# Second layer's MLP: six pairs ahead in shared PSUM banks, low parts behind the next sum, and the second product's weight sums one per step

## The chip, the cores and the metric

The kernel runs on one core of one Trainium2 chip. The metric is the time of one execution in microseconds of device time. The core has a matrix engine (TensorE, PE in the rows; its weight loads are PEld), a vector engine (VectorE, DVE), an activation engine (ScalarE, ACT), a general engine (GpSimd, POOL) and a queue of DMA issues (SyncE, SP). Each engine works through its own instructions in order.

## The reference

A backbone of two layers over 1024 latent tokens of width 1024. Layer 0 mixes tokens by attention, layer 1 by a gated linear attention; each layer ends with a modulated norm and an MLP of width 4096 with squared ReLU. The change touches the MLP of layer 1 alone:

```
h = modulate(rmsnorm(x, g), shift, scale)       # 1024 x 1024
x = x + gate * (relu(h @ w1) ** 2 @ w2)         # w1 1024 x 4096, w2 4096 x 1024
```

All is float32.

## The kernel before

**Numbers in two parts.** For a matmul each f32 operand is split into a rounded high part (`rounded`, a cast on ACT, L164) and a low part, operand minus high part (a subtraction on VectorE, L170). `mm3` (L203 to L205) multiplies high by high, high by low and low by high into one PSUM bank. So a product of 128 outputs over four blocks of 128 is 12 matmuls, 128x512 each.

**Seven products for eight.** `FastMlp` computes both products of the MLP by the Strassen-Winograd scheme: each matrix is cut in 2x2, and from sums of the quarters seven products (steps A11, A12, S1, S2, S3, S4, A22; `STEPS`, L60) are enough. The right-hand operands of the first product are the combinations "11", "21", "22", T1 to T4 of the quarters of the normed input. `combine` (L1216) makes T1 to T4 on VectorE, `shifted` (L1198) makes the others; each is then split. The weight sums S1 = A21 + A22, S2 = S1 − A11, S3 = A11 − A21, S4 = A12 − S2 are made in `add_up` (L1339) on VectorE and split in `prepare` (L1352). Steps A11 and A12, S1 and S2, and so on share sums: `took` (L1291) takes each result out of PSUM, adds what belongs together (`square`, L1274, adds and squares with ReLU on VectorE), subtracts hidden quarters for the second product (`sub`, L1286) and stores them (`store`, L1289) to a buffer `hsp` in DRAM.

**Order.** All engines of this part run in written order (`run`, L1509). There are 16 pairs of 128 hidden columns each.

- `beside` (L1236) makes "11" and "21" for the first half of the norm during the projection before.
- `begin` (L1361): with LEAD = 4 (L70), pairs 0 to 3 run A11 and A12 while the second half of the norm comes in (`norm.begin`, `norm.end`), then S1 and S2 as T1 and T2 become ready. Each product has a PSUM bank of its own; A11's result is copied by ACT (L1299), and VectorE adds it to A12's.
- `first` (L1431): the led pairs' S3, S4, A22, then all seven steps of each pair from 4 on. At fixed distances from the end (`nearly`) it begins to load hidden quarters (`fetch`, L1490) and w2 (`load_rows`, L1467), and to split them.
- `all` (L1516): the second product, four chunks of four pairs by seven steps (`STEPS2`), each step four groups g of 12 matmuls. Behind each group stand, on VectorE, the group before's addition into x (`add`, an STT, L1547) and one piece of the next step's operands (`made`, L1501: `weight`, L1476, then splits W and B). In the S2 step `weight` makes all four sums of a pair (L1481 to L1484).

Of the kernel before, what the change touches and what calls it, by code (L numbers as in the profile page):

```python
# [15 lines left out]
P = 128  # L16
# [45 lines left out]
STEPS2 = STEPS[:5] + (STEPS[6], STEPS[5])  # L62
# [7 lines left out]
LEAD = 4  # L70
# [25 lines left out]
def kernel(  # L96
# [1075 lines left out]
    class FastMlp:  # L1172
# [5 lines left out]
        def __init__(self, l, lead):  # L1178
            self.l, self.lead = l, lead
            self.B = {c: [None] * 4 for c in COMBOS}  # L1180
            self.ts, self.hids = {}, {}
            self.raw, self.sums, self.ops = {}, {}, {}

# [32 lines left out]
        def combine(self, c, j):  # L1216
            b2 = self.norm.ab[0][1][:, j + 4:j + 5]
            (t11, t21), (t12, t22) = [[self.ts[i, j][:, e] for e in range(2)] for i in range(2)]
            v = nc.vector

            if c == "T1":
                self.T[j] = tmp([512], n="T")
                v.tensor_sub(self.T[j], t12, t11)
                split(self.operand(c, j), self.T[j])
            elif c == "T2":
                v.scalar_tensor_tensor(t11, t22, b2, self.T.pop(j), op0=ALU.add, op1=ALU.subtract)
                split(self.operand(c, j), t11)
            elif c == "T3":
                v.scalar_tensor_tensor(t12, t22, self.db[:, j:j + 1], t12, op0=ALU.add, op1=ALU.subtract)
                split(self.operand(c, j), t12)  # L1230
            else:
                v.scalar_tensor_tensor(t21, t21, b2, t11, op0=ALU.add, op1=ALU.subtract)
                split(self.operand(c, j), t21)
                del self.ts[0, j], self.ts[1, j]

        def beside(self, norm, d):  # L1236
# [14 lines left out]
            if d >= 6:  # L1251
                for p in range(self.lead // 2 * (d - 6), self.lead // 2 * (d - 5)):
# [6 lines left out]
        def product(self, ps, w, c, start):  # L1259
            for j in range(4):  # L1260
# [30 lines left out]
        def took(self, p, c, ps):  # L1291

            led = p < self.lead
# [3 lines left out]
            if c == "A11":  # L1297
                h.s1 = h.at("T4") if led else tmp([512], n="s1")
                nc.scalar.copy(h.s1, ps)  # L1299
            elif c == "A12":  # L1300
                h.square("11", ps, h.s1)
            elif c == "S1":
                h.u4 = h.at("T2") if led else tmp([512], n="p5")
                nc.scalar.copy(h.u4, ps)
            elif c == "S2":
# [4 lines left out]
                else:  # L1310
                    h.u2 = tmp([512], n="u2")
                    nc.scalar.copy(h.u2, ps)
# [9 lines left out]
            else:  # L1322
                h.square("21", ps, h.u2 if led else None)
# [28 lines left out]
        def prepare(self, p, c):  # L1352
            t = slot([2, 512], F32R, n="W")
            self.ops[p, c] = (t[:, 0], t[:, 1])
            split(self.ops[p, c], self.sums[p, c] if c[0] == "S" else self.quarter(p, c))
# [5 lines left out]
        def begin(self):  # L1361

            norm, lead = self.norm, self.lead
            self.T = {}

            def early(p):
                w = W.take(min(lead - 1 - p, 1))
                for e, c in ((0, "A11"), (1, "A12")):
                    ps = bank([512])
                    self.product(ps, (w[0][:, e * 512:e * 512 + 512], w[1][:, e * 512:e * 512 + 512]),  # L1370
                                 ("11", "21")[e], True)
                    yield lambda p=p, c=c, ps=ps: self.took(p, c, ps)
# [6 lines left out]
            a0, a1 = early(0)  # L1379
            norm.begin(1)  # L1380
            a0()
            b0, = [next(e1 := early(1))]
            norm.end(1)
            a1()
            b1 = next(e1)
            for j in range(4):
                self.scaled(1, j)
            b0()
            for j in (0, 1):
                self.combine("T1", j)  # L1390
            b1()
            for j in (2, 3):
                self.combine("T1", j)
            for p in range(2, lead):
                late = list(early(p))
                for j in ((4, 5), (6, 7))[p - 2]:
                    self.scaled(1, j)
                for t in late:
                    t()
            self.spill(1)  # L1400
            for p in range(lead):
                self.raw[p, 0] = raws.tile([P, 1024], F32, name=nm("raw"), tag="raw")
                nc.sync.dma_start(self.raw[p, 0][:, :512], w1[self.l, 2 * p][:, :512])

            for p in range(lead):
                t = middle("S1", "T1", p)
                self.combine("T2", p)
# [678 lines left out]
```

## Time and profile before

| | us |
|---|---|
| median of 3 runs | 2946.93 (2946.42 to 2947.62) |
| the profiled execution | 2947.68 |
| its span | 2946.0 |
| first product of this MLP, TensorE | about 2222 to 2576 |
| second product, TensorE | about 2576 to 2928 |

The span is the time from the first to the last instruction that the profile shows; 1.7 us of the execution lie around it. In the rows further down, "busy" counts work, "x" instructions, and the bracket at the end of a row tells how long the engine stood idle before it and which instruction released it. Lines are those of the kernel before.

### The profile page before, as it was taken

The numbers are of one execution on the slowest core, as the hardware profiler recorded it, in microseconds if no ns is written. First come the engines' busy times: TensorE is split into PE (matmuls) and PEld (weight loads), VectorE is DVE, ScalarE is ACT, GpSimd is POOL, SyncE is SP. The second block draws the span as 40 slices with busy tenths as digits, with TensorE's granted clock in tenths as the row PEclk, the third lists the DMA queues.
The fourth block names the chain that finished last, engine by engine and source line by source line (L and its number), as shares of the span: only waits on it lengthen the run. The fifth ranks groups of instructions, "written<-read, shape, count | busy, mean of one in ns | idle before, by whom it ended". The sixth has DMA issues, their size and how long they took to land.

```text
span 2946.0 us, 38543 instructions
## 1 busy us (share of the span) xinstructions
PE 2771.4 (94%) x14728; PEld 2370.0 (80%) x14728; DVE 1985.7 (67%) x3321; ACT 1205.3 (41%) x2353; POOL 661.6 (22%) x600
## 2 busy tenths in 40 slices
PE   5998999999799999999999999999998699999987
PEld 3987899978688888888888889987786588877776
DVE  7858788887877655555455633546766877777776
ACT  4534677773432322321221425875532233333332
POOL 4236455533322422300000100135400111100000
PEclk9999999999899999999999999999999899999998
DMA  6231000044222323311111212334342544553422
GB/s 236 84 103 62 14 15 14 15 140 175 72 79 91 110 86 100 100 51 36 36 43 37 79 55 78 119 139 147 126 164 72 185 150 148 211 217 139 146 83 72
DMA packets 109049, 296.89 MB, mean 101 GB/s; under 512 B 10721, under 2 KB 24161, under 8 KB 108865
## 3 DMA queue, kind: packets, MB, share of 16 engines
q1 hardware_dynamic: 93520, 242.00, 24.3%
q0 software_dynamic: 15344, 52.44, 5.0%
q8 instruction: 115, 1.88, 0.3%
q14 instruction: 70, 0.57, 0.1%
HBM read 229.39 MB, written 65.01 MB: 100 GB/s over the span
## 4 chain that ended last, share of the span: by engine, by line
PE 66%; issue 12%; DVE 12%; ACT 4%; POOL 3%; DMA 2%; SPq 0%; POOLq 0%; DVEq 0%; ACTq 0%
PE b L203 19%; PE b L204 19%; PE b L205 19%; PE b L882 2%; PE b L867 2%; DVE adaj L331 1%; PE b L457 1%; POOL hsp L1289 1%; POOL adaj L317 1%; DMA ada<-in_adaT 1%; DVE wlo L170 1%; DVE B L170 1%; DMA hr<-hsp 1%; DVE h L279 1%; PE b L1749 1%
## 5 line engine op out<-in xcount | busy, mean ns | idle before, releaser
L203 PE MATMUL b<-h,whi 128*128 128x512 f32 (+1 forms) x1544 | 562.8, 366 | 4.3 <-ACT h L164 2.5
L204 PE MATMUL b<-h,whi 128*128 128x512 f32 (+1 forms) x1544 | 560.9, 364 | 3.7 <-DVE h L279 2.2
L205 PE MATMUL b<-h,wlo 128*128 128x512 f32 (+1 forms) x1544 | 560.4, 363 | 4.1 <-DVE wlo L170 4.1
L203 PE MATMUL b<-B,W 128*128 128x512 f32 (+1 forms) x880 | 348.7, 396 | 49.7 <-ACT B L164 25.9
L204 PE MATMUL b<-B,W 128*128 128x512 f32 (+1 forms) x880 | 347.2, 395 | 2.3 <-DVE B L170 2.3
L205 PE MATMUL b<-B,W 128*128 128x512 f32 (+1 forms) x880 | 345.8, 393 | 0.9 <-DVE W L170 0.9
L204 PEld LDWEIGHTS b<-h,whi 128*128 128x128 f32 x1544 | 293.5, 190 | 52.0 <-DVE h L170 3.4
L203 PEld LDWEIGHTS b<-h,whi 128*128 128x128 f32 x1544 | 293.0, 190 | 52.1 <-ACT h L164 4.4
L205 PEld LDWEIGHTS b<-h,wlo 128*128 128x128 f32 x1544 | 293.1, 190 | 51.1 <-DVE wlo L170 6.0
L1153 DVE SCALAR_TENSOR_TENSOR x<-b,mod,x 128x512 f32<-128x512 f32 (+1 forms) x384 | 248.6, 659 | 116.7 <-PE b L205 114.4
L317 POOL TENSOR_TENSOR adaj<-ada,sc 128x1024 f32<-128x1024 f32 x80 | 218.4, 2746 | 383.5 <-PE b L205 186.2
L203 PE MATMUL b<-hid,whi 128*128 128x512 f32 (+1 forms) x768 | 272.9, 355 | 0.0
L204 PE MATMUL b<-hid,whi 128*128 128x512 f32 (+1 forms) x768 | 272.1, 354 | 0.0
L205 PE MATMUL b<-hid,wlo 128*128 128x512 f32 (+1 forms) x768 | 271.9, 354 | 0.0
L203 PEld LDWEIGHTS b<-B,W 128*128 128x128 f32 x880 | 169.9, 193 | 91.1 <-ACT B L164 31.0
L1122 DVE TENSOR_TENSOR relu<-relu 128x512 f32<-128x512 f32 (+1 forms) x96 | 79.6, 835 | 195.3 <-ACT relu L1115 195.3
L204 PEld LDWEIGHTS b<-B,W 128*128 128x128 f32 x880 | 170.0, 193 | 40.7 <-DVE B L170 6.6
L318 ACT ACTIVATE adaj<-adaj 128x1024 f32<-128x1024 f32 x80 | 84.8, 1060 | 288.2 <-POOL adaj L317 288.1
L205 PEld LDWEIGHTS b<-B,W 128*128 128x128 f32 x880 | 169.6, 193 | 35.3 <-DVE W L170 1.6
L170 DVE TENSOR_TENSOR wlo<-raw,whi 128x1024 fp32r<-128x1024 f32 x118 | 150.6, 1283 | 45.4 <-ACT whi L164 43.9
L203 PEld LDWEIGHTS b<-hid,whi 128*128 128x128 f32 x768 | 145.5, 190 | 20.5 <-issue 0.2
L204 PEld LDWEIGHTS b<-hid,whi 128*128 128x128 f32 x768 | 145.4, 189 | 20.3 <-issue 0.2
(284 smaller groups left out, 5632.6 us busy)
## 6 DMA issues: line engine op xcount, KB each, us to landing
raw<-in_w SPq DMA_DIRECT2D x136, 512.0 KB, 3.9
ada<-in_adaT SPq DMA_DIRECT2D x96, 512.0 KB, 4.1
hr<-hsp SPq DMA_DIRECT2D x56, 512.0 KB, 4.5
hsp<-hid POOLq DMA_DIRECT2D x48, 512.0 KB, 4.0
raw<-in_od_win SPq DMA_DIRECT2D x25, 512.0 KB, 3.6
x<-in_xT SPq DMA_DIRECT2D x20, 512.0 KB, 8.2
xsp<-x SPq DMA_DIRECT2D x16, 512.0 KB, 3.3
x<-xsp SPq DMA_DIRECT2D x16, 512.0 KB, 9.1
```

The costliest lines, as they stand in the source:

```text
L170: (lo or nc.vector).tensor_sub(dst[1], src, f(dst[0]))
L203: nc.tensor.matmul(ps, lhsT=ah, rhs=bh, start=start, stop=False, skip_group_check=more)
L204: nc.tensor.matmul(ps, lhsT=ah, rhs=bl, start=False, stop=False, skip_group_check=more)
L205: nc.tensor.matmul(ps, lhsT=al, rhs=bh, start=False, stop=stop, skip_group_check=more)
L279: nc.vector.scalar_tensor_tensor(dst[1], t, b[:, d:d + 1], f(dst[0]), op0=ALU.add, op1=ALU.subtract)
L317: nc.gpsimd.tensor_mul(j, t, sc[w])
L318: nc.scalar.activation(j, j, AF.Copy, accum_out=mod(l, part, w)[:, d:d + 1])
L331: nc.vector.tensor_tensor_reduce(j, t, sc[w], scale=1.0, scalar=0.0, op0=ALU.mult, op1=ALU.add, accum_out=mod(l, part, w)[:, d:d + 1])
L867: nc.tensor.transpose(tb[:, a, b], p[:, o:o + P], ident)
L882: nc.tensor.matmul(av, lhsT=V[self.kts[2 * g + a]][:, h], rhs=self.pts[g][:, a, s], start=(g == 0 and a == 0 and s == 0), stop=(g == ng - ...
L1122: nc.vector.tensor_mul(r, r, r)
L1153: nc.vector.scalar_tensor_tensor(x, ps, gate[i][:, d:d + 1], x, op0=ALU.mult, op1=ALU.add)
```

## The change

`EARLY` pairs (six) run A11 and A12 ahead, and the first `LEAD` of them (three instead of four) S1 and S2 as well. For the early pairs A12 adds to A11 in the same bank, behind ACT's copy of A11; relu and square of that sum are on ACT (L1317, L1318 of the code after). In pairs 3 to 5 VectorE adds A11's copy to S1 and S2 where ACT had copied them. `split` of the class holds the low part back until the next split or product (`flush`). T2, T3, "22" and T4 are made beside other products than before. In the second product the steps come in the order A11, A12, S1, S2, S3, A22, S4; each S step makes one sum in place, and the roundings (`high`) stand one group ahead of the low parts (`low`).

```diff
-LEAD = 4
+EARLY, LEAD = 6, 3
-STEPS2 = STEPS[:5] + (STEPS[6], STEPS[5])
+STEPS2 = tuple(STEPS[i] for i in (0, 1, 3, 2, 4, 6, 5))
...
+        def split(self, dst, src):
+            rounded(nc.scalar, dst[0], src)
+            self.flush()
+            self.low = lambda: nc.vector.tensor_sub(dst[1], src, f(dst[0]))
+
+        def flush(self):
+            if self.low:
+                self.low()
+            self.low = None
...
         def product(self, ps, w, c, start):
+            self.flush()
...
             elif c == "A12":
-                h.square("11", ps, h.s1)
+                if early:
+                    t = tmp([512], n="c")
+                    nc.scalar.activation(t, ps, AF.Relu)
+                    nc.scalar.activation(h.at("11"), t, AF.Square)
+                else:
+                    h.square("11", ps, h.s1)
             elif c == "S1":
                 h.u4 = h.at("T2") if led else tmp([512], n="p5")
-                nc.scalar.copy(h.u4, ps)
+                if early and not led:
+                    nc.vector.tensor_add(h.u4, ps, h.s1)
+                else:
+                    nc.scalar.copy(h.u4, ps)
...
+            two(0, True, (scaled, lambda: self.combine("T1", 3)))
+            two(2, False, (lambda: [self.combine("T2", j) for j in (0, 1)], lambda: [self.combine("T2", j) for j in (2, 3)]))
+            load()
+            two(4, False, (lambda: [second(p) for p in range(2)], lambda: [second(p) for p in range(2, lead)]))
+            self.load_pair(0)
             for p in range(lead):
                 t = middle("S1", "T1", p)
-                self.combine("T2", p)
-                self.add_up(p, "S2")
-                self.prepare(p, "S2")
+                third(p)
                 t()
+            third(3)
+            for s in ("S1", "S2", "S3", "S4"):
+                self.add_up(0, s)
+            self.prepare(0, "S3")
             for p in range(lead):
                 t = middle("S2", "T2", p)
-                self.combine("T3", p)
+                self.combine("T4", p)
                 t()
+            self.combine("T4", 3)
             self.prepare(0, "S4")
             self.prepare(0, "A22")
...
+            v, r = nc.vector, lambda c: self.rows(p, c)
+            if c == "S1":
+                v.tensor_add(r("A21"), r("A21"), r("A22"))
+                return r("A21")
             if c == "S2":
-                self.sums[p] = tmp([512], n="S3") if p % 4 < 2 else slot([512], n="S3")
-                g.tensor_sub(self.sums[p], r("A11"), r("A21"))
-                g.tensor_add(r("A21"), r("A21"), r("A22"))
-                g.tensor_sub(r("A11"), r("A21"), r("A11"))
-                g.tensor_sub(r("A12"), r("A12"), r("A11"))
+                v.tensor_sub(r("A11"), r("A21"), r("A11"))
+                return r("A11")
+            if c == "S3":
+                v.tensor_sub(r("A21"), r("A22"), r("A11"))
+                return r("A21")
+            if c == "S4":
+                v.tensor_sub(r("A12"), r("A12"), r("A11"))
+                return r("A12")
...
-                        if n > 0 and n + 1 < len(jobs):
-                            make(n + 1, g)
+                        if not last:
+                            high(*((n + 1, g + 1) if g < 3 else (n + 2, 0)))
+                            low(n + 1, g)
```

`two(p, between, beside)` runs A11 of pairs p and p + 1 and then A12 of both, with `norm.begin` and `norm.end` behind the first and the second A11 where `between` is set, and the two functions of `beside` behind the two A12; `third(j)` makes T3 and "22" of block j; `second(p)` makes and splits S2 of pair p.

VectorE in the second product of the first chunk, in the step that prepares S2. A name such as raw_22476 is a buffer of w2 with its number, x the residual, b a PSUM bank, hr hidden quarters. Before:

```order
L1547 SCALAR_TENSOR_TENSOR x_22656<-b_22735,mod_11711,x_22656 128x512
L1481 TENSOR_TENSOR S_22776<-raw_22476 128x512
L1482 TENSOR_TENSOR raw_22476<-raw_22476,raw_22552 128x512
L1483 TENSOR_TENSOR raw_22476<-raw_22476 128x512
L1484 TENSOR_TENSOR raw_22552<-raw_22552,raw_22476 128x512
L170 TENSOR_TENSOR W_22781<-raw_22476,W_22781 128x512
L170 TENSOR_TENSOR B_22784<-hr_22672,B_22784 128x512
L1547 SCALAR_TENSOR_TENSOR x_22656<-b_22736,mod_11711,x_22656 128x512
```

After:

```order
L1606 SCALAR_TENSOR_TENSOR x_22623<-b_22728,mod_11711,x_22623 128x512
L1524 TENSOR_TENSOR raw_22464<-raw_22464 128x512
L1556 TENSOR_TENSOR W_22803<-raw_22462,W_22803 128x512
L1556 TENSOR_TENSOR B_22805<-hr_22721,B_22805 128x512
L1606 SCALAR_TENSOR_TENSOR x_22633<-b_22813,mod_11711,x_22633 128x512
```

Four sums stood between two STTs, now one (L1524); the low part behind it (L1556) is that of the pair before (raw_22462), not of the sum just made.

ACT at the start of the MLP, from its copy of pair 0's A11 on; whi is the high part of a first-layer weight, T a difference that becomes B. Before:

```order
L1299 COPY hid_20116<-b_20081 128x512
L164 CAST whi_20120<-raw_20118 128x1024
L1299 COPY hid_20163<-b_20124 128x512
L164 CAST B_20167<-T_20165 128x512
L164 CAST B_20172<-T_20170 128x512
L164 CAST B_20180<-T_20178 128x512
L164 CAST B_20185<-T_20183 128x512
L164 CAST whi_20190<-raw_20188 128x1024
L1299 COPY hid_20222<-b_20194 128x512
```

After:

```order
L1313 COPY hid_20102<-b_20080 128x512
L164 CAST whi_20106<-raw_20104 128x1024
L1313 COPY hid_20125<-b_20110 128x512
L164 CAST B_20147<-T_20145 128x512
L164 CAST B_20154<-T_20152 128x512
L164 CAST B_20162<-T_20160 128x512
L1317 ACTIVATE c_20169<-b_20080 128x512
L1318 ACTIVATE hid_20102<-c_20169 128x512
L164 CAST B_20187<-T_20185 128x512
L1317 ACTIVATE c_20189<-b_20110 128x512
L1318 ACTIVATE hid_20125<-c_20189 128x512
L164 CAST whi_20194<-raw_20192 128x1024
```

The whi that stood behind the four B belonged to the fourth pair; in the changed code the fourth pair's stands ahead of them, and the one behind them is the fifth pair's. Two pairs of relu and square are new.

ACT where T4 is made (B from t) and the first pair's sums are rounded (W from S). Before:

```order
L164 CAST B_20478<-t_19894 128x512
L164 CAST B_20482<-t_19899 128x512
L164 CAST B_20486<-t_19933 128x512
L164 CAST B_20490<-t_19938 128x512
L164 CAST W_20509<-S_20505 128x512
```

After:

```order
L164 CAST W_20446<-S_20442 128x512
L164 CAST B_20464<-t_19894 128x512
L164 CAST B_20483<-t_19899 128x512
L164 CAST B_20502<-t_19933 128x512
L164 CAST B_20507<-t_19938 128x512
L164 CAST W_20510<-S_20444 128x512
```

Before, the first pair's W of S3 and S4 had been rounded ahead of T4 and the next in line was a W of the second pair; now S3's W (W_20446) stands ahead of T4 and S4's (W_20510) behind it.

## Rows read from the trace of the kernel before

**Rows 1.** The page's first part: busy us, share of the span, instructions.

```profile
PE 2771.4 (94%) x14728; PEld 2370.0 (80%) x14728; DVE 1985.7 (67%) x3321; ACT 1205.3 (41%) x2353; POOL 661.6 (22%) x600
```

**Rows 2.** Busy time by stretch: us, engines' busy us (x instructions), clock, DMA share, GB/s.

```profile
2240.00:2350.00 110.00, 75.02 (x287) 58.22 (x287) 90.27 (x139) 30.02 (x50) 10.52 (x16) 0.84 0.35 124
2350.00:2576.00 226.00, 226.00 (x999) 187.15 (x998) 169.64 (x263) 74.87 (x139) 30.49 (x45) 1.00 0.49 172
2576.00:2596.00 20.00, 20.00 (x90) 16.39 (x88) 16.64 (x26) 3.15 (x6) 2.71 (x4) 1.00 1.06 396
2596.00:2615.00 19.00, 12.50 (x35) 8.30 (x35) 15.84 (x25) 8.25 (x16) 0.00 (x0) 0.73 0.46 169
...
2680.00:2700.00 20.00, 15.46 (x50) 11.06 (x49) 16.72 (x26) 9.07 (x17) 0.00 (x0) 0.74 0.45 158
2766.00:2785.00 19.00, 14.26 (x53) 10.42 (x52) 16.99 (x27) 8.68 (x17) 0.00 (x0) 0.82 0.50 167
2850.00:2870.00 20.00, 12.36 (x39) 8.74 (x38) 16.95 (x27) 10.09 (x19) 0.00 (x0) 0.74 0.16 53
```

**Rows 3.** TensorE's waits, 2150 to 2946 us: total us, times, longest us.

```profile
PE b L203 <- ACT B L164: 25.9, 10, 4.6
PE b L203 <- DVE c L1282: 16.3, 4, 10.6
PE b L203 <- ACT whi L164: 7.8, 1, 7.8
```

**Rows 4.** Timeline of VectorE in a step with four sums: start, us, instruction.

```profile
2686.44 0.74 DVE L1547 SCALAR_TENSOR_TENSOR x<-b,mod,x 128x512 f32<-128x512 f32 x1
2687.11 0.68 DVE L1481 TENSOR_TENSOR S<-raw 128x512 f32<-128x512 f32 x1
...
2689.98 0.69 DVE L170 TENSOR_TENSOR W<-raw,W 128x512 fp32r<-128x512 f32 x1
2690.59 0.69 DVE L170 TENSOR_TENSOR B<-hr,B 128x512 fp32r<-128x512 f32 x1
2691.19 0.74 DVE L1547 SCALAR_TENSOR_TENSOR x<-b,mod,x 128x512 f32<-128x512 f32 x1
```

**Rows 5.** Timeline of ACT in the same step.

```profile
2689.33 0.62 ACT L164 CAST W<-raw 128x512 fp32r<-128x512 f32 x1 [3.61 <-DVE raw L1483]
```

**Rows 6.** Timeline of TensorE in the last step of the second product.

```profile
2909.90 0.38 PE L203 MATMUL b<-B,W 128*128 128x256 f32 x1 [1.91 <-ACT B L164]
```

**Rows 7.** Timeline of VectorE, a low part of first-layer weights.

```profile
2233.36 1.22 DVE L170 TENSOR_TENSOR wlo<-raw,whi 128x1024 fp32r<-128x1024 f32 x1 [0.74 <-ACT whi L164]
```

**Rows 8.** Timeline of VectorE, the low part of one T4 and the next T4.

```profile
2300.28 0.69 DVE L170 TENSOR_TENSOR B<-t,B 128x512 fp32r<-128x512 f32 x1 [0.74 <-ACT B L164]
2300.89 0.74 DVE L1232 SCALAR_TENSOR_TENSOR t<-t,mod 128x512 f32<-128x512 f32 x1
```

**Rows 9.** Timeline of TensorE, three of its four waits for c.

```profile
2308.38 0.77 PE L203 MATMUL b<-B,W 128*128 128x512 f32 x1 [10.64 <-DVE c L1282]
2320.94 0.47 PE L203 MATMUL b<-B,W 128*128 128x512 f32 x1 [2.77 <-DVE c L1282]
2331.92 0.47 PE L203 MATMUL b<-B,W 128*128 128x512 f32 x1 [0.95 <-DVE c L1282]
```

**Rows 10.** Timelines of ACT (square, copy) and of VectorE (sum, square).

```profile
2222.89 0.64 ACT L223 ACTIVATE sq<-x 128x512 f32<-128x512 f32 x1 [2.12 <-DVE x L1030]
2247.92 0.58 ACT L1299 COPY hid<-b 128x512 f32<-128x512 f32 x1
2234.51 0.68 DVE L1282 TENSOR_TENSOR c<-b,hid 128x512 f32<-128x512 f32 x1
2235.22 0.69 DVE L1283 SCALAR_TENSOR_TENSOR hid<-c 128x512 f32<-128x512 f32 x1
```

**Rows 11.** Timeline of ACT behind the seam, and the page's DMA landing of x (last figure, us).

```profile
2590.91 0.62 ACT L164 CAST B<-hr 128x512 fp32r<-128x512 f32 x1 [2.77 <-DMA hr<-hsp]
x<-xsp SPq DMA_DIRECT2D x16, 512.0 KB, 9.1
```

More of the change, by code (lines that the diff above doesn't have):

```diff
@@ L1251, in beside @@
             if d >= 6:
-                for p in range(self.lead // 2 * (d - 6), self.lead // 2 * (d - 5)):
+                for p in range(2 * (d - 6), min(2 * (d - 5), self.lead)):
                     self.raw[p, 1] = slot([1024], n="raw")
@@ L1291, in took @@
         def took(self, p, c, ps):
-            led = p < self.lead
+            led, early = p < self.lead, p < self.early
             if p not in self.hids:
@@ L1322, in took @@
             else:
-                h.square("21", ps, h.u2 if led else None)
+                h.square("21", ps, h.u2 if led else h.s1 if early else None)
                 h.store(3, 1)
@@ L1361, in begin, with opened, closed @@
         def begin(self):
-            norm, lead = self.norm, self.lead
+            norm, lead, E = self.norm, self.lead, self.early
             self.T = {}
[L1366 to L1372, printed above, removed]
+            def opened(p):
+                w = W.take(min(E - 1 - p, 2))
+                ps = bank([512])
+                self.product(ps, (w[0][:, :512], w[1][:, :512]), "11", True)
+                return w, ps
+            def closed(p, w, ps):
+                self.product(ps, (w[0][:, 512:], w[1][:, 512:]), "21", False)
+                return lambda: self.took(p, "A12", ps)
             def middle(c, b, p):
@@ L1377, in middle @@
                 return lambda: self.took(p, c, ps)
[L1379 to L1403, printed above, removed]
+            def two(p, between, beside):
+                a = opened(p)
+                if between:
+                    norm.begin(1)
+                self.took(p, "A11", a[1])
+                b = opened(p + 1)
+                if between:
+                    norm.end(1)
+                self.took(p + 1, "A11", b[1])
+                t = closed(p, *a)
+                del a
+                beside[0]()
+                t()
+                t = closed(p + 1, *b)
+                del b
+                beside[1]()
+                t()
@@ new lines, in scaled, with load @@
+            def scaled():
+                for j in range(4):
+                    for e in range(2):
+                        self.scaled(1, j + 4 * e)
+                    if j:
+                        self.combine("T1", j - 1)
+                self.spill(1)
+                self.norm.xs = self.xs = None
+            def load():
+                for p in range(lead):
+                    self.raw[p, 0] = raws.tile([P, 1024], F32, name=nm("raw"), tag="raw")
+                    nc.sync.dma_start(self.raw[p, 0][:, :512], w1[self.l, 2 * p][:, :512])
@@ L1433, in first @@
             steps = [(p, c) for p in range(NP) for c, _, _ in STEPS
-                     if p >= self.lead or c in ("S3", "S4", "A22")]
+                     if p >= self.early or c in ("S3", "S4", "A22") or (p >= self.lead and c[0] == "S")]
             todo, n = [], 0
@@ L1944 @@
     W.add(*[lambda d=d: load_w(od_wout[d]) for d in range(ND)])
-    W.add(*[lambda p=p: load_w(w1[1, 2 * p]) for p in range(LEAD)])
+    W.add(*[lambda p=p: load_w(w1[1, 2 * p]) for p in range(EARLY)])
     mixed = [[None] * ND for _ in TCS]
```

93 lines of the change are left out of this document (51 added, 42 removed).

## The prediction

> **What bounds the kernel now.** I read the page first: TensorE is busy 94% of the span, VectorE 67% [rows 1]. A saving can then come only from places where TensorE stands still, so I asked for busy time by stretch and for what ended TensorE's waits. In the reader's place, look at the count of matmuls in each stretch and not only at the busy time, because slow matmuls count as busy. From 2350 to 2576 us TensorE runs 999 matmuls in 226 us without a hole; two of them are cut by the edges, so the pitch is 226 / 997 = 0.2267 us, a product of 12 takes 2.72 us and a step of the second product (48) 10.88 us. Against that pitch the beginning of the MLP, 2240 to 2350 us, has 287 matmuls in 110 us: 110 − 287 × 0.2267 = **44.9 us lost**. Four windows in the second product lose 19 − 35 × 0.2267 = 11.1, 20 − 50 × 0.2267 = 8.7, 19 − 53 × 0.2267 = 7.0 and 20 − 39 × 0.2267 = 11.2 us: **38.0 us lost** [rows 2]. In these windows the mean granted clock is 0.73 to 0.84 of full speed, in the dense ones 1.00: after a stop of some us the matmuls first go at the lower of the two levels, 1.2 GHz, so a stop costs more than it lasts (44.9 us for 35.0 idle in the beginning, 38.0 for 23.4 in the four windows).
>
> The waits name the causes [rows 3]. In the second product it is ACT's rounding of the operand B, 25.9 us in ten waits; in the beginning it is a sum that VectorE reads out of PSUM (c, 16.3 us in four) and a rounding of first-layer weights (whi, 7.8).
>
> **The second product.** The step in which all four weight sums stand costs VectorE, for one of its four groups, from one STT to the next: 0.67 for the STT, 2.87 for four sums (0.72 each), 0.61 and 0.60 for two low parts, 4.75 us [rows 4]; TensorE needs 2.72. Four groups are 19.0 against 10.9 us, 8.1 more than TensorE has, four times (one for each chunk of pairs). ACT adds nothing of its own: its rounding of W waits 3.61 us for the third sum [rows 5], and TensorE waits for the B behind it. In the changed code every group of S1, S2, S3 and S4 has one sum: 0.67 + 0.72 + 0.61 + 0.60 = 2.60 us, and the other three steps 1.88. That is below 2.72 with **0.12 us to spare**. The roundings also stand one group ahead of their low parts, so VectorE doesn't wait for ACT's answer, and TensorE's next step needs a low part three groups after it was made. The in-place chain S1, S2, S3, S4 lies over four steps, each link over ten us behind the one before. Nothing that I find is late next. So −38.0 us. The wait of 1.91 us for ACT's B at the last step [rows 6] comes from the same lack of lead and goes too: −1.9.
>
> **The beginning.** What is computed is the same; VectorE has 10 instructions less in all, ACT 3 more. Three things move.
>
> First, six pairs instead of four run A11 and A12 ahead, 12 products or 32.6 us of TensorE work instead of 8 or 21.8. Rounding and low part of each weight are taken up to two pairs ahead. This removes the 7.8 us wait on whi: in ACT's order the rounding that TensorE waited for stood behind four roundings of T1, now it stands ahead of them. It also gives T2 and the S2 sums time, so that the S1 and S2 products find their operands. In their place I see two short waits. Two 1024-wide low parts now stand ahead of VectorE's small step in the norm (one before), at 1.2 us each [rows 7], which holds the norm's broadcast matmul by 1.7 us. And A12 now goes into the bank of A11, so it must wait for ACT's copy of A11; for the third pair that copy stands behind roundings of 0.6 and 1.05 us, 2.6 us late.
>
> Second, the low part is issued behind the next sum. Before, each T4 took 0.74, 0.74 of waiting for ACT and 0.61 for the low part, 2.09 us on VectorE [rows 8]; now 0.74 + 0.61 = 1.35. Four T4 take 5.4 and not 8.4 us; with T1, T2, T3 and the three S2 this is some 12 us of VectorE's time. But the rounding of S4's weight sum is queued behind all four T4 roundings on ACT, and TensorE has only S3's product (2.7 us) to cover it. Counted on from about 2222: 19 products, 2 us of norm matmuls and the 4.3 of waits put the end of S3 at 2222 + 51.7 + 6.3 = 2280.0, that of the third S1 at 2269.1. Behind ACT's copy of that S1 and two roundings, about 2271, VectorE has four sums and two low parts (2.6 + 1.2), three times a T4, the two sums of an S2 and a low part (3 × 2.6), and the last T4 (0.74): 2283.4; ACT's start and two roundings (0.6 each) end at 2285.3. So S4 waits 5.3 us, with 2.8 of lower clock as at such a stop before: 8.1.
>
> Third, only three led pairs run S3, S4, A22 in a row. Such a triple is 8.16 us of TensorE, but the times at which a later bank is freed lie 2320.94 − 2308.38 = 12.6 and 11.0 us apart [rows 9], because sums, low parts, squares and differences of a pair fill VectorE there at 0.60 to 0.75 us each. Two intervals of this kind are left for three. As estimates from these intervals I take 2.2 us at the first A22, 6.5 + 2.3 at the second, and at S3 of the three pairs that follow 2.9 + 1.5, 1.7 and 1.7, since for these VectorE adds A11's sum at S1 and S2 where ACT copied. Their four products take 10.9 us, and about 13.6 with S1 and S2, as VectorE does.
>
> My sum after: 1.7 + 2.6 + 8.1 + 2.2 + 8.8 + 4.4 + 3.4 = 31.2 us for 44.9 before, **−13.7**. This is the weakest term. Its ends: 0, if each wait only changes its place, and −28, if S4's wait and the second A22's are each covered.
>
> For the six A12 the change puts relu and square on ACT, where VectorE did an addition and a square. Rows: a copy out of PSUM takes ACT 0.58 and a square 0.64 [rows 10], VectorE's sum and square of the led pairs 0.68 and 0.69. So six of these give VectorE 8.2 us in a stretch where it is the one waited for, and ACT takes 7.3.
>
> The Trainium skill, "ScalarE: Activation LUTs", section "Rules for kernel authors", says the opposite: relu and add belong on VectorE, which it calls up to about three times as fast per element in bf16. By that rule the six would better have stayed, the −13.7 would shrink by up to 8.2 to −5.5, and the sum would be 2903.5. These f32 rows don't show VectorE faster, so the forecast follows them; the rule's outcome is rival (f).
>
> **The seam.** Where the first product ends, the loads of eight x tiles, w2 and the hidden states come together; 2576 to 2596 us move 396 GB/s with the engines' share at 1.06 [rows 2]. A rounding of B waited 2.77 us for its hidden state there [rows 11], which TensorE hardly felt. The changed code asks for the same bytes in some 14 us less time, and the first STT waits for x with low parts queued behind it on VectorE. From 0 (all hidden, as before) to 9 us (one landing of x [rows 11], with nothing to cover it); I take +2, since the 2.77 us are the nearest row.
>
> **Sum.** 2947.7 − 38.0 − 1.9 − 13.7 + 2 = 2896.1 for an execution like the profiled one. That one lies 0.75 us above the median of the runs, so **2895.3 us**.
>
> **Rivals.**
> (a) Only the second product gains. The beginning swaps its waits one for one, since VectorE is the bound in both codes. For it: VectorE is busy 90.3 of these 110 us [rows 2]. Against it: T4 alone gives back 3 us. Time: 2895.3 + 13.7 = 2909.0. Chance 0.22.
> (b) The second product stays bound by VectorE. The margin of 0.12 us holds only if no instruction waits for ACT. If one answer of 0.74 us is waited for in each of the 16 groups of a chunk, a group takes 3.34, and 64 × (3.34 − 2.72) = 40 us come back: about 2934. Against it: roundings are a group ahead in the order. Chance 0.06.
> (c) Slower. Hidden states come late. Rounding and low parts now want their data one group sooner, and a slot for a load is freed only by the low part that read the one before. If every one of the 28 steps waits 2.77 us, as the row shows once, that is 77.6 us, and 2895.3 + 77.6 = 2973. It decides from 1.8 us in each step (51.6 / 28). Against it: in the dense stretches of the second product before, no such wait reaches TensorE, and two steps of loads are still on their way. Chance 0.06.
> (d) The change doesn't do what it says: TensorE's holes are put elsewhere and the time stays at 2947. The order of the instructions speaks against it: the sums do stand one in a group. Chance 0.04.
> (e) The beginning gains its full 28 us: 2881. Chance 0.10.
> (f) ACT is late instead: relu and square of six pairs, 7.3 us, stand ahead of the roundings that TensorE waits for in the beginning, and the exchange costs what it was to save. For it: ACT's queue is in order, and the copies that A12 waits for stand in it too. Against it: ACT is busy 30.0 of the 110 us. Time: 2895.3 + 8.2 = 2903.5. Chance 0.06.
>
> **How the numbers follow.** The forecast, 2895.3 with 2885 to 2903 around it, has 0.46; with (a) to (f) the chances sum to 1. The range runs from (e) with the seam at nothing, 2881 − 2 = 2879, to (a) with the seam at its far end and a fifth of (b), 2909 + 7 + 8 = 2924. It leaves out most of (b), (c) and (d). A measurement of this kernel can tell about 0.2%, 6 us. Faster 0.89: forecast, (a), (e), (f) and nearly all of (b) end below 2941. Same 0.05: (d) and a little of (b). Slower 0.06: (c).
>
> **What would show it.** In the profile after: no wait of TensorE on B between the seam and the last step, 10.9 us a step with the clock at 1.00; STTs 2.72 us apart with one sum behind each; no wait on whi; in the beginning one wait on W at S4 of about 5 us and one on c at the second A22, some 31 us lost in the windows; the first product ending near 2562. The prediction is wrong if S4's rounding comes in time or twice as late, if a step of the second product is longer than 11 us, or if the third or fourth step of the second product waits for loads.

## The result, and the profile after

The changed kernel takes 2905.24 us (median of 4 runs, 2902.06 to 2907.66) against 2946.68 us before on the same chip: a ratio of 0.9859, 95% interval 0.9842 to 0.9876. That is 41.4 us less. The forecast was 2895.3 us with a range of 2879 to 2924; the measured time lies in the range, and outside the 2885 to 2903 us that the prediction set around its forecast. The profiled execution of the code after took 2907.66 us, with a span of 2906.0.

TensorE's record holds the 2736 product matmuls of this MLP in both traces, so number 1, number 1345 and number 2641 mark the same places: the start of the first product, of the second, and of its last step. Between these marks (us):

| stage | before | after | difference | forecast |
|---|---|---|---|---|
| start of this MLP, from the start of the span | 2221.9 | 2225.7 | +3.8 | 0 |
| first product | 351.7 | 343.6 | −8.1 | −13.7 |
| second product, 27 steps | 332.9 | 296.3 | −36.6 | −38.0 + 2 |
| its last step | 21.3 | 22.2 | +0.8 | −1.9 |
| the rest | 18.1 | 18.1 | 0.0 | 0 |

The sum of the last four lines is −43.8, and −40.0 with the first, which is the difference of the two spans. The first line belongs to single executions: the instructions ahead of this MLP are the same on every engine, and in the 14 profiles of this study it starts anywhere from 2216.6 to 2225.7 us.

First the busy time of the kernel after by stretch (us, then TensorE, its weight loads, VectorE, ACT and GpSimd with their instructions, granted clock, DMA share, GB/s), which answers to [rows 2]:

```profile
2240.00:2345.00 105.00, 83.74 (x326) 66.73 (x325) 78.76 (x121) 37.14 (x62) 8.29 (x12) 0.89 0.35 123
2345.00:2375.00 30.00, 26.48 (x116) 21.35 (x115) 26.00 (x41) 5.82 (x10) 5.45 (x8) 1.00 0.57 193
...
2569.00:2575.00 6.00, 4.88 (x22) 3.73 (x21) 5.97 (x10) 4.75 (x9) 2.71 (x4) 1.00 1.05 395
...
2600.00:2860.00 260.00, 259.73 (x1145) 214.39 (x1145) 220.86 (x349) 110.99 (x202) 0.00 (x0) 1.00 0.37 132
```

From 2600 to 2860, most of the second product, TensorE stands still for 0.27 us, at a clock of 1.00. The four long steps are gone: they took 22.3, 19.8, 18.3 and 22.3 us before, and the steps in their places take 11.2, 10.88, 10.88 and 11.4 us now. The beginning still loses 105 − 326 × 0.2267 = 31.1 and 30 − 116 × 0.2267 = 3.7 us.

TensorE's waits after (total us, times, longest), which answer to [rows 3]:

```profile
PE b L203 <- DVE u L1335: 8.4, 3, 4.9
PE b L203 <- DVE c L1296: 7.8, 2, 5.6
PE b L203 <- ACT W L164: 6.5, 1, 6.5
PE b L232 <- DVE acc L224: 6.2, 2, 4.9
PE b L204 <- DVE B L1556: 5.4, 4, 2.7
PE b L245 <- DVE acc L236: 4.7, 3, 2.0
PE b L203 <- ACT hid L1313: 2.2, 1, 2.2
```

The 25.9 us for ACT's rounding of B and the 7.8 for whi have disappeared. New are u (VectorE's addition for pairs 3 to 5), hid (ACT's copy of A11) and four waits for a low part of B, of which one lies at the seam, one is 0.2 us and two lie in the last step. The wait for W is S4's rounding; before, there was one for another rounded weight sum (at 2288.76), which [rows 3] leaves out:

```profile
PE b L203 <- ACT W L164: 7.5, 1, 7.5
```

VectorE in a step that makes one sum for each group, against [rows 4] (timeline: start, us, instruction, idle time before it):

```profile
2631.07 0.75 DVE L1606 SCALAR_TENSOR_TENSOR x<-b,mod,x 128x512 f32<-128x512 f32 x1 [0.17 <-PE b L205]
2631.74 0.68 DVE L1530 TENSOR_TENSOR raw<-raw,raw 128x512 f32<-128x512 f32 x1
2632.34 0.68 DVE L1556 TENSOR_TENSOR W<-raw,W 128x512 fp32r<-128x512 f32 x1
2632.94 0.68 DVE L1556 TENSOR_TENSOR B<-hr,B 128x512 fp32r<-128x512 f32 x1
2633.79 0.75 DVE L1606 SCALAR_TENSOR_TENSOR x<-b,mod,x 128x512 f32<-128x512 f32 x1 [0.17 <-PE b L205]
```

2.72 us from STT to STT, of which 0.17 us are left over waiting for TensorE. Before it was 4.75 us.

### The profile page after: what moved, and what is told of

Same layout as the page of the kernel before. It is cut to its first block, busy times and chain, and to the rows that moved or that the text cites. A ratio compares the mean times of both kernels' runs of the same rounds, so it can differ in the third digit from the quotient of the medians.

```text
span 2906.0 us, 38558 instructions
## 1 busy us (share of the span) xinstructions
PE 2760.6 (95%) x14728; PEld 2366.6 (81%) x14728; DVE 1975.3 (68%) x3311; ACT 1210.9 (42%) x2356; POOL 659.8 (23%) x600
## 3 DMA queue, kind: packets, MB, share of 16 engines
q1 hardware_dynamic: 93520, 242.27, 24.6%
## 4 chain that ended last, share of the span: by engine, by line
PE 75%; DVE 11%; issue 5%; ACT 4%; POOL 2%; DMA 2%; SPq 0%; POOLq 0%; DVEq 0%; ACTq 0%
PE b L203 22%; PE b L205 22%; PE b L204 22%; PE b L882 2%; PE b L867 2%; PE b L457 1%; DVE adaj L331 1%; POOL adaj L317 1%; DVE wlo L170 1%; DMA ada<-in_adaT 1%; DVE acc L224 1%; DVE h L279 1%; PE b L1809 1%; ACT sq L223 1%; PE b L1765 1%
## 5 line engine op out<-in xcount | busy, mean ns | idle before, releaser
L203 PE MATMUL b<-B,W 128*128 128x512 f32 (+1 forms) x864 | 338.5, 392 | 22.6 <-DVE u L1335 8.4
L204 PE MATMUL b<-B,W 128*128 128x512 f32 (+1 forms) x864 | 337.6, 391 | 5.5 <-DVE B L1556 5.4
L205 PE MATMUL b<-B,W 128*128 128x512 f32 (+1 forms) x864 | 336.6, 390 | 0.0
L203 PEld LDWEIGHTS b<-B,W 128*128 128x128 f32 x864 | 165.1, 191 | 57.9 <-ACT W L164 12.9
L204 PEld LDWEIGHTS b<-B,W 128*128 128x128 f32 x864 | 165.4, 191 | 41.0 <-DVE B L1556 7.6
L205 PEld LDWEIGHTS b<-B,W 128*128 128x128 f32 x864 | 165.1, 191 | 33.6 <-DVE W L1189 0.3
```

Of the source, the lines that this page charges most:

```text
L203: nc.tensor.matmul(ps, lhsT=ah, rhs=bh, start=start, stop=False, skip_group_check=more)
L204: nc.tensor.matmul(ps, lhsT=ah, rhs=bl, start=False, stop=False, skip_group_check=more)
L205: nc.tensor.matmul(ps, lhsT=al, rhs=bh, start=False, stop=stop, skip_group_check=more)
```

## The experiments

Each kernel ran beside the kernel before on one chip. Where stages are given, they are measured between the marks above. The kernel after, profiled again, gave 343.8, 297.8, 23.0 and 18.2 us: the first product repeats to 0.2 us, the others to 1.5, while its runs spread over 6.5 us. So single terms are read from stages, and ratios from runs.

**The two parts apart.** `x1_second_only` is the kernel before with `STEPS2`, `weight`, `made` and `all` of the kernel after; `x2_begin_only` is the kernel after with these four of the kernel before.

> The beginning of the kernel before with the second product of the kernel after. If the two parts are independent, the second product's 27 full steps take 296 us as in the kernel after (333 before), the first product 352 us as before, and the time is 2946.7 - 36.6 + 0.8 = about 2911 us. If the gain of the second product rests on the new beginning (hidden quarters stored earlier, other buffers free), it comes out between 2911 and 2947, with waits at the seam.

> The beginning of the kernel after with the second product of the kernel before. If independent: first product 343.6 us (351.7 before), second product 333 us with its four long steps, time about 2946.7 - 8.1 = 2938.6 us. If the beginning only swaps waits and the 8 us are an accident of one execution: within 2 us of 2946.7.

The second product alone: 2912.8 us, ratio 0.988 (0.9865 to 0.9895); first product 351.9, 27 steps 297.0, last step 22.8 us. The beginning alone: 2941.58 us, ratio 0.9976 (0.9961 to 0.9991); first product 344.1, 27 steps 331.2, last step 20.9 us. Both parts keep their size without the other. The beginning's gain is real and small: 7.6 us by the stage.

**What the second product needed.** `x3_no_lead` puts each low part right behind its rounding again, and the first operands ahead of the seam back to about their old places:

```diff
-                rounded(nc.scalar, t[:, 0], a)
-                both.append((t[:, 0], t[:, 1], a))
+                split((t[:, 0], t[:, 1]), a)
+                both.append(t)
...
-                        if not last:
-                            high(*((n + 1, g + 1) if g < 3 else (n + 2, 0)))
-                            low(n + 1, g)
+                        if n > 0 and n + 1 < len(jobs):
+                            make(n + 1, g)
```

> The kernel after, but each low part stands directly behind its rounding, as in the kernel before; the weight sums stay one per step. If the lead of the roundings is needed (VectorE then waits 0.74 us for ACT's answer in each group with a sum: 3.34 us against TensorE's 2.72), the 16 steps that prepare a sum take about 13.4 us and the time is about 2905 + 40 = 2945 us. If spreading the sums alone is the gain, the steps stay at 10.9 us and the time is 2905 to 2908 us.

`x4_four_sums` keeps the lead and puts the four sums of a pair back into one step:

```diff
-STEPS2 = tuple(STEPS[i] for i in (0, 1, 3, 2, 4, 6, 5))
+STEPS2 = STEPS[:5] + (STEPS[6], STEPS[5])
...
             if c == "S2":
-                v.tensor_sub(r("A11"), r("A21"), r("A11"))
-                return r("A11")
+                self.sums[p] = tmp([512], n="S3") if p % 4 < 2 else slot([512], n="S3")
+                g.tensor_sub(self.sums[p], r("A11"), r("A21"))
+                g.tensor_add(r("A21"), r("A21"), r("A22"))
+                g.tensor_sub(r("A11"), r("A21"), r("A11"))
+                g.tensor_sub(r("A12"), r("A12"), r("A11"))
...
```

> The kernel after, but with the old order of steps and all four weight sums of a pair in the step that prepares S2; the lead of the roundings stays. If VectorE's four sums are the cause of the long steps (4.75 us a group against 2.72), each chunk loses its 8.1 us again and some slow clock: 2905 + 32 to 38 = 2937 to 2943 us, with four steps of 19 to 22 us. If the waiting for ACT was the cause, the steps stay near 11 us and the time is near 2906 us.

Without the lead: 2936.75 us, ratio 0.9958 (0.9942 to 0.9975), 27 steps 323.1, last step 27.7 us. With the lead and four sums: 2932.39 us, ratio 0.9946 (0.9931 to 0.9961), 27 steps 327.4, with long steps of 18.4, 17.5, 18.6 and 20.7 us. VectorE without the lead:

```profile
2597.19 0.74 DVE L1606 SCALAR_TENSOR_TENSOR x<-b,mod,x 128x512 f32<-128x512 f32 x1
2597.85 0.68 DVE L1524 TENSOR_TENSOR raw<-raw 128x512 f32<-128x512 f32 x1
2599.22 0.69 DVE L170 TENSOR_TENSOR W<-raw,W 128x512 fp32r<-128x512 f32 x1 [0.69 <-ACT W L164]
2599.82 0.69 DVE L170 TENSOR_TENSOR B<-hr,B 128x512 fp32r<-128x512 f32 x1
2600.43 0.75 DVE L1606 SCALAR_TENSOR_TENSOR x<-b,mod,x 128x512 f32<-128x512 f32 x1
```

The sum is followed by 0.69 us of waiting for ACT's answer to it, and the group takes 3.24 us: too long for TensorE's 2.72. Of the sixteen steps that were expected at 13.4 us, seven take 13.0 to 13.3, seven 11.3 to 11.6 and two more than 15 us. With four sums and the lead, a group takes 4.64 us on VectorE (from 2673.09 to 2677.73), and TensorE waits for the low part of B:

```profile
PE b L204 <- DVE B L1551: 21.6, 10, 4.8
```

So neither half is the gain. x2, with the same beginning and the old second product, has 331.2 us for the 27 steps; spreading alone takes them to 323.1 us (−8.1), the lead alone to 327.4 (−3.8), both to 296.3 (−34.9). The reason is the sum over a chunk: sixteen groups that are 0.52 us too long make 8.3 us, four that are 1.92 us too long make 7.7, and the four of the kernel before, 2.03 too long, made 8.1. Only both edits together bring a group under 2.72 us. VectorE's waiting for ACT is no cause in the kernel before, whose long groups have no idle time on VectorE [rows 4]; it appears where a single sum is followed by its own low part, and the lead removes it.

**The last step.** In `x5_pool_acc` the sums of squares for the next norm are added on GpSimd up to the last step:

```diff
-                            accs[key] = sumsq(accs[key], xs[i][d][:, p0:p1], p1 - p0)
+                            accs[key] = sumsq(accs[key], xs[i][d][:, p0:p1], p1 - p0, nc.gpsimd if n + 1 < len(jobs) else None)
```

> The kernel after, but the additions of squares for the next norm are on GpSimd instead of VectorE ahead of the last step. If the waits for B at the last step (1.40 and 2.69 us) come from VectorE doing an addition of x, a square's sum, a weight sum and two low parts for each group of the step before (3.9 us against 2.72), they go, and the last step takes 16 to 18 us instead of 22.2: about 2900 us. If low parts are late because of the loads or of ACT, the last step stays at 22 us and the time at 2905 us.

2897.29 us, ratio 0.9836 (0.9819 to 0.9852). The last step took 18.3 instead of 22.2 us, of the two waits for B (4.1 us) one of 0.4 us was left, and the wait for the sum of squares (acc) at the norm's first matmul grew from 1.3 to 2.3 us:

```profile
PE b L232 <- POOL acc L224: 2.3, 1, 2.3
```

The kernel after shows the cause on VectorE, in the step ahead of the last, and its effect on TensorE:

```profile
2863.99 0.74 DVE L1606 SCALAR_TENSOR_TENSOR x<-b,mod,x 128x512 f32<-128x512 f32 x1
2865.49 0.69 DVE L224 TENSOR_TENSOR acc<-acc,sq 128x512 f32<-128x512 f32 x1 [0.76 <-ACT sq L223]
2866.11 0.68 DVE L1530 TENSOR_TENSOR raw<-raw,raw 128x512 f32<-128x512 f32 x1
2866.71 0.68 DVE L1556 TENSOR_TENSOR W<-raw,W 128x512 fp32r<-128x512 f32 x1
2867.31 0.68 DVE L1556 TENSOR_TENSOR B<-hr,B 128x512 fp32r<-128x512 f32 x1
2867.91 0.74 DVE L1606 SCALAR_TENSOR_TENSOR x<-b,mod,x 128x512 f32<-128x512 f32 x1
```

```profile
2868.04 0.39 PE L204 MATMUL b<-B,W 128*128 128x256 f32 x1 [1.40 <-DVE B L1556]
...
2871.36 0.58 PE L204 MATMUL b<-B,W 128*128 128x256 f32 x1 [2.69 <-DVE B L1556]
```

A group takes 3.92 us there: in the last chunk the step that runs A22 finishes parts of x, so a square's addition with a wait of 0.76 us for ACT is added, and the change has put S4's weight sum into that very step. Before, all sums of a chunk were made in its second step.

x5 doesn't bring these groups down to 2.60 us. Its low part of B lasts 1.2 to 1.8 us beside GpSimd's additions, and a group still takes 3.0 to 3.6 us:

```profile
2849.66 0.74 DVE L1606 SCALAR_TENSOR_TENSOR x<-b,mod,x 128x512 f32<-128x512 f32 x1
2850.32 0.68 DVE L1530 TENSOR_TENSOR raw<-raw,raw 128x512 f32<-128x512 f32 x1
2850.92 0.68 DVE L1556 TENSOR_TENSOR W<-raw,W 128x512 fp32r<-128x512 f32 x1
2851.52 1.78 DVE L1556 TENSOR_TENSOR B<-hr,B 128x512 fp32r<-128x512 f32 x1
2853.22 0.74 DVE L1606 SCALAR_TENSOR_TENSOR x<-b,mod,x 128x512 f32<-128x512 f32 x1
```

**The beginning.** `x6_dve_square` puts relu and square of the six early A12 on VectorE:

```diff
-                    nc.scalar.activation(t, ps, AF.Relu)
-                    nc.scalar.activation(h.at("11"), t, AF.Square)
+                    nc.vector.tensor_scalar(t, ps, 0.0, 0.0, op0=ALU.max, op1=ALU.add)
+                    nc.vector.tensor_mul(h.at("11"), t, t)
```

> The kernel after, but relu and square of the six early A12 are on VectorE (two instructions each). If VectorE is what the beginning waits for, the twelve instructions lengthen the first product by part of their 8.2 us, from 343.6 to 346 to 352 us: 2907 to 2913 us. If VectorE is the better place for them (rule of the page on activation tables; ACT late, rival f), the first product gets shorter, to 336 to 343 us.

First product 346.8 us, 3.2 us more than after (2905.81 us by the runs, too close to tell from the kernel after by them). A wait of 1.7 us for a rounded S2 sum appears. Rival (f) falls. ACT's relu and square take 0.59 and 0.63 us here, VectorE's in x6 0.68 and 0.69, and VectorE's queue is the one waited for: in this stage ACT is the better place. The Trainium skill, "ScalarE: Activation LUTs", section "Rules for kernel authors", would have the six on VectorE, with a figure for bf16; for these f32 tiles the trace doesn't agree, by the 3.2 us.

`x7_s4_first` moves one line, `self.prepare(0, "S4")`, ahead of the four T4.

> The kernel after, but S4's first weight sum is rounded ahead of the four T4. If the place behind T4 in ACT's order is the cause of the 6.45 us wait, this wait goes; but A22 needs T4 one product (2.72 us) later, so a wait of about 3.7 us appears there, and the 5.6 us wait of the second A22 stays: the first product takes 340 to 342 us instead of 343.6, the time 2901 to 2904 us. If VectorE's amount of work alone sets the pace, the first product stays within 1 us of 343.6.

First product 343.6 us, as after (2904.03 us, ratio 0.9857, 0.9839 to 0.9874). The wait on W was gone, and the waits on c had taken all of it (those of TensorE, 2215 to 2380 us):

```profile
PE b L203 <- DVE c L1296: 15.8, 2, 10.2
PE b L203 <- DVE u L1335: 8.1, 3, 4.6
```

So the place of S4's rounding, which the prediction named as the cause of the wait, sets where TensorE waits and not how long in all.

`x8_pool_add` frees the banks of S1 and S2 of pairs 3 to 5 by an ACT copy and adds A11's copy on GpSimd:

```diff
+                nc.scalar.copy(h.u4, ps)
                 if early and not led:
-                    nc.vector.tensor_add(h.u4, ps, h.s1)
-                else:
-                    nc.scalar.copy(h.u4, ps)
+                    nc.gpsimd.tensor_add(h.u4, h.u4, h.s1)
...
+                    nc.scalar.copy(h.u2, ps)
                     if early:
-                        nc.vector.tensor_add(h.u2, ps, h.s1)
-                    else:
-                        nc.scalar.copy(h.u2, ps)
+                        nc.gpsimd.tensor_add(h.u2, h.u2, h.s1)
```

> The kernel after, but for pairs 3 to 5 ACT copies S1 and S2 out of their banks and GpSimd adds A11's copy, so VectorE has six additions less and the banks are free sooner. If the three waits for u (4.88, 1.76 and 1.76 us, with some 5 us of slow clock) come from these additions standing in VectorE's queue, they go: first product 332 to 336 us, time 2894 to 2898 us. If VectorE is behind by then anyway, the waits only move to c at the next bank and the first product stays above 341 us.

First product 338.4 us, 5.3 less than after, 2899.5 us (ratio 0.9839, 0.9822 to 0.9857). The three waits for u (4.88, 1.76, 1.76) became waits for c of 1.99, 1.21 and 1.21. The expected 8 to 12 us came to half. Between the marks of the first product VectorE has six instructions less than in the kernel after, and is busy longer: 267.0 us for 262.8.

**Together, and more of it.** `x9_pool_both` joins the edits of x5 and x8. `x10_pool_subs` adds to it the differences of hidden quarters of the led pairs and one addition of S2 on GpSimd, `x11_pool_sums` the first pair's four weight sums:

```diff
-                nc.vector.tensor_sub(self.at(c), self.at(a), self.at(b))
+                eng = nc.gpsimd if self.p < LEAD else nc.vector
+                eng.tensor_sub(self.at(c), self.at(a), self.at(b))
...
-                    nc.vector.tensor_add(h.u4, h.u4, h.u2)
+                    nc.gpsimd.tensor_add(h.u4, h.u4, h.u2)
...
-                self.add_up(0, s)
+                self.add_up(0, s, nc.gpsimd)
```

> The kernel after itself, beside the three that follow. If the 3.8 us by which its first profile starts this MLP later belong to one execution (the streams ahead of it are the same), the MLP starts anywhere between 2217 and 2226 us, and the stages repeat: first product 343.6, 27 steps 296.3, last step 22.2, tail 18.2 us. If the change delays what is ahead of it, the start is again near 2225.7 us.

> The kernel after with two edits tried singly: squares' sums ahead of the last step on GpSimd, and A11's addition for pairs 3 to 5 as ACT copy and GpSimd addition. If VectorE's load in two separate places is the cause, the gains add: first product 338.4, last step 18.3 us, 3.9 + 5.3 = 9.2 us less than the kernel after, about 2896 us. If GpSimd or its memory port gets in VectorE's way, less than 7 us.

> As the one before, and for the three led pairs the four differences of hidden quarters and one addition of S2's sum are on GpSimd. If VectorE's amount of work sets the pace of the led pairs, each pair gives back 5 x 0.65 = 3.3 us: the waits at S4 (6.45), at the second A22 (5.6) and at S3 of the fourth pair shrink, and the first product takes 328 to 332 us, the time about 2888 us. If slots of hidden quarters (held longer, 1.3 us for each GpSimd instruction) or their stores set the pace, the first product stays at 337 us or above.

> As the one before, and the first pair's four weight sums are on GpSimd too. They then no longer stand behind T3 in VectorE's order, and VectorE has 2.6 us less ahead of S4's rounding: the wait at S4 shrinks by about as much, first product 325 to 330 us. If S4's sum comes later from GpSimd (four dependent instructions at 1.3 us), the wait grows instead.

The kernel after again: 2904.77 us, ratio 0.9852 (0.9832 to 0.9871), with this MLP starting at 2222.8 us. x9: **2894.52 us, ratio 0.9822 (0.9805 to 0.9839)**, first product 338.2, last step 19.8 us: by the median the fastest of the study, 10.3 us below the kernel after on the same chip by the medians, 8.9 by these two stages. x10: 2897.76 us (0.9835, 0.982 to 0.985), first product 343.7 us. x11: 2897.74 us (0.9832, 0.9816 to 0.9848), first product 344.2 us; 328 to 332 and 325 to 330 us had been expected for these two. Taking more work off VectorE lost the 5.6 us of the beginning again. VectorE and then GpSimd in x9 show what such work costs:

```profile
2345.02 0.69 DVE L1369 TENSOR_TENSOR S<-S,raw 128x512 f32<-128x512 f32 x1
2345.62 3.62 DVE L1371 TENSOR_TENSOR S<-raw,raw 128x512 f32<-128x512 f32 x1
2349.17 0.68 DVE L1373 TENSOR_TENSOR S<-raw,S 128x512 f32<-128x512 f32 x1
```

```profile
2346.13 1.31 POOL L1335 TENSOR_TENSOR u<-u,hid 128x512 f32<-128x512 f32 x1
2347.38 1.30 POOL L1325 TENSOR_TENSOR p<-p,hid 128x512 f32<-128x512 f32 x1
```

An instruction of VectorE that takes 0.68 us elsewhere lasts 3.62 us while GpSimd's two additions run, and ends 0.56 us after them. Both of its inputs lie in SBUF. The same line at 2360.74 lasts 3.62 us again, beside the next two additions. Instructions with an input from PSUM keep their time: no L1296 runs beside such an addition in x9, but two do in x10 and take 0.68 and 0.69 us, and four additions into x do in x5 and take 0.74 or 0.75. So two additions on GpSimd saved VectorE 2 × 0.68 us and cost it 2.9. What x8 gained did not come from a lighter VectorE; that leaves ACT's copy, which frees the bank, though no run has this copy without GpSimd. In x10 and x11 fifteen and nineteen more instructions stand on GpSimd, and VectorE loses more than it is spared: in the first product it is busy 270.2 and 270.0 us, for 267.1 in x9. Three of its instructions in x10:

```profile
2326.09 2.44 DVE L1370 TENSOR_TENSOR S<-S,raw 128x512 f32<-128x512 f32 x1
...
2329.05 2.38 DVE L1374 TENSOR_TENSOR S<-raw,S 128x512 f32<-128x512 f32 x1
2331.36 3.63 DVE L1189 TENSOR_TENSOR W<-raw,W 128x512 fp32r<-128x512 f32 x1
```

Whether the later differences and stores on GpSimd, the other side of x10's expectation, have a part in the 5.6 us is not shown: no run separates the two. The Trainium skill, "SBUF — State Buffer", section "Who interferes with whom", states this as a rule: a VectorE instruction with two inputs in SBUF contends with a GpSimd instruction that reads SBUF. The trace agrees, with 0.68 to 3.62 us.

## Why the prediction was right, and where it was not

About 11.5 us lie between the profiled 2907.66 us and the 2896.1 of the sum: 5.6 in the beginning, 2.7 in the last step, 3.8 ahead of the changed code and −0.6 in the 27 steps. Two of the prediction's own signs of being wrong came, in small: the steps of 12.3, 11.2, 11.4 and 11.3 us are longer than 11, and the third step waits for a load.

**The second product: right, step by step.** The excess of the four steps was 39.2 us by the steps (22.3 + 19.8 + 18.3 + 22.3 − 4 × 10.88) and is gone. The 0.12 us left over in a group were 0.17. The chain of in-place sums brought no wait, nor did the order of the steps ahead of the last chunk. Rival (b), waiting for ACT, did not occur, and x3 shows that it would have: 3.24 us a group where the prediction reckoned 3.34. Rival (c), late hidden states, occurred once and small. Behind the seam ACT's rounding of B waited 5.04 us for its load, where before it had been 2.77 [rows 11], and VectorE 3.02 us for ACT; the third step took 11.2 us for it (12.6 in the second profile). No later step waits for a load. ACT's row:

```profile
2586.13 0.62 ACT L164 CAST B<-hr 128x512 fp32r<-128x512 f32 x1 [5.04 <-DMA hr<-hsp]
```

**The seam: right.** Forecast +2; the first and third step take 1.4 and 0.3 us longer than 10.88 (1.4 and 1.7 in the second profile). The first waits 1.1 us for a low part of B, which stands behind the first product's last squares and differences on VectorE; the third is the late load just named.

**The last step: wrong in sign.** The failing step of the prediction is "comes from the same lack of lead and goes too: −1.9" [rows 6]. It went from ACT's B to VectorE's low B and grew to 4.1 us. The sums of squares were left out of VectorE's sum for that step: with them a group costs 3.92 and not 2.60 us. x5 shows it by taking them off VectorE (−3.9 us). Those of the last chunk's A12 cost the two steps behind it 0.5 and 0.4 us, which x5 also removes.

**The beginning: right in direction and mechanism of the first part, mis-sized in all.** −8.1 for −13.7. The waits themselves were placed well:

| wait | forecast | measured |
|---|---|---|
| norm's broadcast matmul | 1.7 | 1.2 |
| A12 of the third pair | 2.6 | 2.2 |
| S4 of the first pair | 5.3 | 6.5 |
| first A22 | 2.2 | 2.2 |
| second A22 | 6.5 | 5.6 |
| S3 of pairs 3, 4, 5 | 2.9, 1.7, 1.7 | 4.9, 1.8, 1.8 |

They sum to 24.6 and 26.0 us. The rest of the miss is the clock, the term of the sum that was mis-sized. The first product of the kernel after has 343.6 − 1344 × 0.2267 − about 2 for the norm's matmuls = 37 us above the dense pitch, 11 more than the waits, and the prediction had put 6.6 for it: 2.8, 2.3 and 1.5 at three stops. In the trace four stops (S4, first and second A22, S3 of pair 3) are each followed by 8 to 13 matmuls at 0.43 us, the pitch of the 1.2 GHz level, 0.2 us too long each; behind the stop of 5.6 us the granted clock is 0.50 from 2312.8 to 2318.4. The stop at the first A22, 2.2 us, begins right behind the slow stretch of S4, and 8 slow matmuls follow it; stops of 1.8 and 2.2 us in a stretch at full clock are followed by none. Two of the stops:

```profile
2289.76 0.80 PE L203 MATMUL b<-B,W 128*128 128x512 f32 x1 [6.45 <-ACT W L164]
2312.79 0.77 PE L203 MATMUL b<-B,W 128*128 128x512 f32 x1 [5.60 <-DVE c L1296]
```

The list of waits that the prediction started from was incomplete: of the ten for ACT's B one, 2.1 us, lies in the beginning, and the 7.5 us for W are left out. That the six pairs, the late low part and the three led pairs each have a share in the 8.1 us is not shown, since x2 runs them together.

One reason given for these waits was also too simple. "Sums, low parts, squares and differences of a pair fill VectorE there" holds for the kernel before, where VectorE is busy 35.8 of the 38 us from 2308 to 2346. In the kernel after it is busy 32.2 of the 39.8 us from 2297.1 to 2336.9. Its in-order queue stands at low parts whose roundings have not come, and ACT's roundings wait for something else. ACT and VectorE in the kernel after:

```profile
2301.74 0.62 ACT L164 CAST W<-raw 128x512 fp32r<-128x512 f32 x1 [6.10 <-PE b L205]
2307.28 0.62 ACT L164 CAST W<-S 128x512 fp32r<-128x512 f32 x1 [4.92 <-PE b L205]
...
2325.76 0.62 ACT L164 CAST W<-S 128x512 fp32r<-128x512 f32 x1 [3.96 <-DMA hsp<-hid]
```

```profile
2302.39 0.69 DVE L1189 TENSOR_TENSOR W<-raw,W 128x512 fp32r<-128x512 f32 x1 [2.90 <-ACT W L164]
...
2326.42 0.69 DVE L1189 TENSOR_TENSOR W<-S,W 128x512 fp32r<-128x512 f32 x1 [2.56 <-ACT W L164]
```

The rounding has its input and waits for the end of a product (PE) or of a store (hsp): for a buffer to be written into, as I read it. x7 fits this: with S4's rounding moved, the first product stayed at 343.6 us to 0.1. That more buffers would shorten it is argued and not shown: no run had more.

**Rivals (a), (e), (f), (d).** (a), at 2909.0, lies nearer to the measured 2905.2 than the forecast, but its mechanism fell: x2 shows that the beginning gains by itself. Its number came near by the misses just listed. (e) did not occur. (f) fell by x6, (d) by the stages.

**The start.** 3.8 us of the profiled difference lie ahead of the changed code, in one execution. The kernel after again started this MLP 2.9 us earlier with the same code.

## What to carry to other kernels

Where an engine works for another at a fixed beat, count its work for each beat with every visitor included (sums of squares, a wait for an answer), and add up what is too long over the whole period: sixteen beats too long by a fifth add up to about as much as four too long by three quarters, and neither of two cures gave a quarter of what both gave. Spread periodic work over the beats, but look at the last period, where other work joins. Moving work off a loaded VectorE onto GpSimd has a price where GpSimd reads SBUF beside two-input instructions of VectorE: in x5 and x8 the move was worth it, in x10 and x11 not. What x8 saved seems to be the earlier free PSUM bank more than VectorE's instructions.

## What the runs showed of the hardware

Two additions of 1.30 us on GpSimd stretched one VectorE subtraction from 0.68 to 3.62 us, while VectorE instructions with an input from PSUM kept their 0.69 and 0.74 us beside such additions. After a stop of 4.9 to 6.5 us TensorE ran 11 to 13 matmuls at 0.43 us; after one of 1.8 us in a dense stretch, none in the kernel after, but in x6 eight after stops of 1.7 and 0.4 us close together. The start of this MLP varies by 9 us between profiles of kernels that are the same up to there; nearly 8 of them have arisen by 320 us, where the mean granted clock so far is 0.94 to 0.96 from profile to profile.
